# Output-gate projection first; q and k projected beside the Fourier stage and read back by the scan stage

## The chip, the cores and the metric

One core of one Trainium2 chip runs the whole kernel in one launch. The metric is the device time of that launch in microseconds (us). TensorE (PE) does the matmuls, VectorE (DVE), ScalarE (ACT) and GpSimd (POOL) the rest, and SyncE (SP) issues almost all of the transfers.

## What is computed

One encoder layer on x of 2048 positions by 1024 channels, in float32. One projection of x gives q, k (256 channels each), v (512), two gate inputs of rank 16, an output gate z_gla (512), u (512) and a second output gate z_fnet (512):

```python
proj = jnp.einsum('bsd,de->bse', x, w_in[l])
q, k, v, gf_lr, gb_lr, z_gla, u, z_fnet = jnp.split(proj, _OFFSETS, axis=-1)
```

Two branches follow. The first is gated linear attention: log decays per key channel come from the low-rank gates through log-sigmoid, a running sum of them scales q and k, and a scan over chunks goes once forward and once backward; the sum is RMS-normalised and multiplied by silu(z_gla). The second takes the real part of a two-dimensional Fourier transform of u (positions by channels in four groups), a small matrix per group, and multiplies by silu(z_fnet). Both go through one output projection, then `x <- LayerNorm(alpha * x + y)`.

## The kernel before

**Precision.** Every float32 operand of a large product is split into a rounded high part and the remainder (`split`, L53 to L59): ACT casts the high part (L56), and another engine, DVE unless the caller names one, subtracts it for the low part (L59). A product is then three matmuls: high by high, high by low, low by high. `load_x` (L72) loads one block of x, 256 positions, in two halves and splits them into two tiles `xhl` (four buffers in all, so two blocks); `proj_t` (L83) and `proj_n` (L90) run a projection of a block, the first with channels on the partitions, the second with positions there.

**Stage 1** (`phase1`, L137): the projections to u and z_fnet, in a seven-product (Strassen-like) form. A pair of 256-position blocks has fourteen products of 24 matmuls each (`run`, `product`, L304), and there are four pairs. The weights of a product are sums of quarters of the weight matrix, so someone has to form these sums and split them: `w_sums` (L170) does it, for u on DVE and for z_fnet on POOL. The order of the start is written out in `first`: pair 0 and the first products of pair 1 are woven together while weights and sums arrive. At the end of the stage the weights of the output gate z_gla are loaded and split into the buffer `wC`.

**Stage 2** (`phase2`, L424): the Fourier transform (a radix stage on DVE and POOL, L447 to L459; small matmuls L552 and L572; the product with silu(z_fnet) on POOL, L587), woven with the projection of z_gla, `zg_block` (L527): per block 96 matmuls (L87) out of `wC`, silu and scale on ACT, a store to DRAM. x comes by `load_x(b, nc.gpsimd)`: its low part is subtracted on POOL. The weights of v and of the gates are loaded into `wA` (L644, L645).

**Stage 3** (`phase3`, L661), called the scan stage below, goes over eight blocks. In block b it projects gates and v (`pw_part`, `pv_part`, L94), turns the gates into running sums and exponentials (`gates`: a matmul L722, ACT L724 to L727, DVE L728, two scans L733 and L735 over 64 partitions each, DVE L739 and L740, ACT L750 and L751), projects q and k (`qk`, 96 matmuls L87 out of `wB`), and multiplies them by the exponentials straight out of PSUM (`scaled`, L758, eight DVE operations of 64 partitions). For the block before, `gla_a` forms masked scores (PE L773 and L774, a transpose L777, a mask and a predicated copy on DVE, L779 and L780) and `gla_b` the state update and the inner output (PE L790 and L797). `chain_f` carries the state from chunk to chunk in two steps on POOL (L982, L985). x is loaded again, its low part now on DVE.

**Stage 4** (`phase4`): the output projection (L1006), norms and stores.

Each engine works through its own queue in order; the order within a queue is set by a scheduler that works from the program's order and from when buffers come free.

## Time and profile before

| | |
|---|---|
| median of 3 runs | 825.47 us (825.43 to 826.39) |
| span of the profiled execution | 823.8 us |
| PE busy | 768.0 us (93%) |
| DVE busy | 554.5 us (67%) |
| ACT busy | 352.8 us (43%) |
| POOL busy | 283.9 us (34%) |
| mean granted TensorE clock | 0.977 |
| moved by DMA | 110.57 MB |

The span runs from the first to the last instruction on the core; the median lies 1.7 us above it. The times are device times, and the three runs lie within 1 us. A busy PE is not always a useful PE: at the lower of its two clocks the same matmul counts twice the time.

### The profile page before, as it was taken

To read this page: it belongs to the slowest core of one execution; us is meant where nothing else is said; L and a number is where in the kernel's file an instruction comes from. 1 tells how busy PE (TensorE), PEld (TensorE's weight loads), DVE (VectorE), ACT (ScalarE), POOL (GpSimd) and SP (SyncE) were. 2 spreads that over 40 slices of the span, in tenths; PEclk is the share of its full clock that TensorE was granted. 3 is DMA by queue.
4 is the path that set the end of the run, shared out by engine and by line. 5 is a ranking of instruction groups with operands and counts; after the bars stand their busy time and mean duration, and the time that the engine had idled before them with its cause. 6 is when DMAs were issued, how large, how long until landed. Compare 5 with 4: busy or idle time off the path is not lost.

```text
span 823.8 us, 13935 instructions
## 1 busy us (share of the span) xinstructions
PE 768.0 (93%) x5542; PEld 721.3 (88%) x5542; DVE 554.5 (67%) x814; ACT 352.8 (43%) x635; POOL 283.9 (34%) x194
## 2 busy tenths in 40 slices
PE   6787999998859899989999999999998999999995
PEld 6787999998859799979999999999986788888884
DVE  4997757448997742357764765765775877677664
ACT  4632333235335455454344434443564343443441
POOL 0874212134446357601112111111243645545421
PEclk9999999999979999989999999999999999999998
DMA  8333552258645466762112112112165554455222
GB/s 289 105 100 123 168 166 65 94 170 249 181 130 170 131 183 184 236 204 77 53 52 103 53 52 103 52 53 78 52 200 195 194 178 160 151 175 179 88 92 81
DMA packets 61824, 110.57 MB, mean 134 GB/s; under 512 B 6228, under 2 KB 36948, under 8 KB 61751
## 3 DMA queue, kind: packets, MB, share of 16 engines
q1 hardware_dynamic: 61750, 109.60, 40.3%
q8 instruction: 45, 0.74, 0.4%
q14 instruction: 29, 0.23, 0.1%
HBM read 77.08 MB, written 32.51 MB: 133 GB/s over the span
## 4 chain that ended last, share of the span: by engine, by line
PE 50%; DMA 2%; DVE 1%; issue 1%; POOL 1%; ACT 1%; SPq 0%; POOLq 0%; DVEq 0%
PE mm L1006 19%; PE mm L87 11%; PE mm L94 10%; PE pa L773 2%; PE pg L797 2%; PE pg L790 2%; PE pa L1046 1%; DMA zg<-zg_d 1%; PE pg L777 1%; DMA wraw<-in_w_out_dram 1%; PE mm L722 1%; PE pg L1058 0%; PE pg L1059 0%; DMA qp<-q_d 0%; POOL zg L1065 0%
## 5 line engine op out<-in xcount | busy, mean ns | idle before, releaser
L982 POOL TENSOR_TENSOR S<-S 64x512 f32<-64x512 f32 x30 | 39.5, 1318 | 215.5 <-ACT S L792 210.7
L87 PE MATMUL mm<-xhl,wC_w 128*128 128x256 f32 x768 | 99.9, 290 | 2.9 <-POOL xhl L59 2.9
L94 PE MATMUL mm<-wA_w,xhl 128*128 128x272 f32 x768 | 101.2, 290 | 0.0
L87 PEld LDWEIGHTS mm<-xhl,wC_w 128*128 128x128 f32 x768 | 97.4, 199 | 3.6 <-POOL xhl L59 3.1
L1006 PE MATMUL mm<-wB_w,mix 128*128 128x512 f32 (+1 forms) x396 | 94.8, 389 | 3.5 <-ACT mix L56 2.4
L94 PEld LDWEIGHTS mm<-wA_w,xhl 128*128 128x128 f32 x768 | 97.6, 188 | 0.0
L87 PE MATMUL mm<-xhl,wB_w 128*128 128x256 f32 x768 | 97.1, 288 | 0.0
L87 PEld LDWEIGHTS mm<-xhl,wB_w 128*128 128x128 f32 x768 | 95.3, 196 | 0.0
L1006 PE MATMUL mm<-wA_w,mix 128*128 128x512 f32 (+1 forms) x396 | 92.9, 388 | 0.0
L1006 PEld LDWEIGHTS mm<-wB_w,mix 128*128 128x128 f32 x396 | 73.4, 191 | 20.4 <-ACT mix L56 3.1
L1006 PEld LDWEIGHTS mm<-wA_w,mix 128*128 128x128 f32 x396 | 71.6, 188 | 13.6
L304 PE MATMUL mm<-wC_s,x 128*128 128x256 f32 x384 | 54.2, 299 | 12.3 <-DVE x L58 4.4
L304 PEld LDWEIGHTS mm<-wC_s,x 128*128 128x128 f32 x384 | 50.8, 203 | 14.2 <-ACT wC_s L56 4.4
L1094 POOL TENSOR_TENSOR r<-r,lnb 128x1024 f32<-128x1024 f32 x15 | 35.9, 2391 | 78.2 <-issue 51.2
L59 POOL TENSOR_TENSOR xhl<-xraw,xhl 128x1024 fp32r<-128x1024 f32 x16 | 41.8, 2621 | 45.0 <-ACT xhl L56 36.0
L56 ACT CAST xhl<-xraw 128x1024 fp32r<-128x1024 f32 x32 | 33.4, 1047 | 40.8 <-PE mm L94 22.1
L59 DVE TENSOR_TENSOR x<-xraw,x 128x1024 fp32r<-128x1024 f32 (+1 forms) x29 | 39.5, 1374 | 13.5 <-ACT x L56 13.4
L56 ACT CAST x<-xraw 128x1024 fp32r<-128x1024 f32 (+1 forms) x28 | 26.9, 979 | 42.3 <-PE mm L304 22.8
L985 POOL TENSOR_TENSOR S<-S,alpha 64x512 f32<-64x512 f32 x30 | 36.4, 1214 | 2.4
L758 DVE TENSOR_TENSOR kp<-g,mm 64x512 f32<-64x512 f32 x32 | 21.9, 686 | 22.3 <-PE mm L87 20.9
L304 PE MATMUL mm<-x,wB_s 128*128 128x256 f32 x288 | 36.4, 283 | 0.0
L304 PEld LDWEIGHTS mm<-x,wB_s 128*128 128x128 f32 x288 | 35.4, 192 | 0.0
(195 smaller groups left out, 1463.1 us busy)
## 6 DMA issues: line engine op xcount, KB each, us to landing
xraw<-in_xt_dram SPq DMA_DIRECT2D x47, 512.0 KB, 4.6
xr<-in_x_dram SPq DMA_DIRECT2D x16, 512.0 KB, 3.8
out_dram<-r SPq DMA_DIRECT2D x15, 512.0 KB, 2.8
zg_d<-zs SPq DMA_DIRECT2D x32, 128.0 KB, 3.9
zfl<-zf_d SPq DMA_DIRECT2D x32, 128.0 KB, 3.0
mf_d<-yf SPq DMA_DIRECT2D x16, 256.0 KB, 2.4
wraw<-in_w_out_dram SPq DMA_DIRECT2D x16, 256.0 KB, 3.4
mf<-mf_d SPq DMA_DIRECT2D x8, 512.0 KB, 4.4
```

The source lines that it names most:

```text
L56: nc.scalar.copy(out=hi, in_=src)
L59: (lo_eng or nc.vector).tensor_tensor(out=lo, in0=src, in1=f32(hi), op=ALU.subtract)
L87: self.nc.tensor.matmul(ps, w[:, s, k, c0:c0 + P], x[:, m, k % 4, :], start=(k == 0 and i == 0), stop=(k == KB - 1 and i == 2))
L94: self.nc.tensor.matmul(ps, x[:, s, k % 4, t * P:(t + 1) * P], w[:, m, k, c0:c0 + cols], start=(k == 0 and i == 0), stop=(k == KB - 1 and ...
L304: nc.tensor.matmul(ps[:, i], s_[s][:, k, i * P:(i + 1) * P], m_[m][:, k], start=(k == 0 and j == 0), stop=(k == 3 and j == 2))
L758: V.tensor_tensor(out=o[ds, par::2], in0=e[ds, par::2], in1=ps[64 * par:64 * par + 64], op=ALU.mult)
L773: nc.tensor.matmul(af[:, h], k[0:64, h, ts_], q[0:64, h, ts_], start=True, stop=True)
L790: nc.tensor.matmul(up[:, h * P:(h + 1) * P], ks[:, h], v[:, h * P:(h + 1) * P], start=True, stop=True)
L982: E.tensor_tensor(out=S[ds, dst], in0=S[ds, dst], in1=S[ds, src], op=ALU.add)
L985: E.tensor_tensor(out=d3, in0=d3, in1=al, op=ALU.mult)
L1006: nc.tensor.matmul(y, c["mix"][:, s, eb], w[:, v, eb % 4, lo:lo + m], start=(eb == 4 and i == 0), stop=(eb == 3 and i == 2))
L1094: nc.gpsimd.tensor_tensor(out=r, in0=r, in1=lnb, op=ALU.add)
```

## The change

**Stage 1** begins with the output-gate projection. `zg_first` loads block 0 of x and the gate's weights piece by piece and runs 96 matmuls (L229) as the pieces come; `zg_block` runs the other seven blocks (672 matmuls, L87) with silu, scale and store. Beside them `w_prep` forms and splits the sums of the Strassen weights, now all on DVE; only the last four sums wait (`w_late`) until the buffer `wA`, which holds the gate's weights, is free. Then the four pairs run one after the other in the same order, and the woven start is gone. The weights of q and k are loaded into `wC` at the end of stage 1.

**Stage 2** weaves the projection of q and k (`qk_block`, 768 matmuls) where that of z_gla stood. The result is copied from PSUM by ACT and stored in DRAM by DMAs that ACT issues, instead of silu, scale and a store by SP.

**Stage 3** no longer projects q and k. Four DMAs per block (`qk_load`) bring them back, each row onto both partition halves; `scaled` becomes two DVE operations of 128 x 1024 elements whose operands both lie in SBUF (L777). x is loaded further ahead, its low part on POOL. The order of the rest is another: both gate projections first, then the gates, the earlier block's scores, and the v projections between them. Blocks 0 and 1 have their v projections earlier.

The number of matmuls is the same; 768 of them change place with 768 others.

```diff
+            def w_prep(rp):
...
+                for u in range(2):
...
+                    w_split(u, 1, RW[u, 0])
+                    yield
+                    w_split(u, 2, RW[u, 2])
+                    yield
+                    for h in range(2):
+                        sub(T[h], r(1, h), r(0, h))
+                        sub(T[2 + h], r(3, h), T[h])
+                    yield
+                    w_half(u, 6, 1)
...
+            def zg_first():
+                w = self.wzg = self.wpool.tile([P, 2, KB, 512], F32R, name="wA_w", tag="wA")
...
+                for k in range(KB):
...
+                    nc.sync.dma_start(out=xr[:, k % 4], in_=a["xt"][0, :, k])
+                    raw = self.xpool.tile([P, 512], F32, name="wraw", tag="wraw", bufs=4)
+                    nc.sync.dma_start(out=raw, in_=a["w_zg"][:, k])
...
+                    self.split(x[:, 0, k % 4], x[:, 1, k % 4], xr[:, k % 4])
+                    self.split(w[:, 0, k], w[:, 1, k], raw)
...
+                ps = zg_first()
+                xn = self.load_x(1)
+                for c in range(4):
+                    zg_out(0, c, ps[c], rp)
+                for b in range(1, NBLK - 1):
+                    xh, xn = xn, self.load_x(b + 1)
+                    zg_block(b, xh, bg, rp)
...
-            for p, c in first(xs[0], xs[1]):
-                for u in range(2):
-                    run(u, c, p, xs[p])
...
+            nxt = x_prep(0, xs[0])
+            zg_block(NBLK - 1, xn, nxt, st)
+            w_late()
+            for p in range(NP):
...
-                        self.wzg = self.load_w("wC", a["w_zg"], KB, 512)
+                        self.wqk = self.load_w("wC", a["w_qk"], KB, 512)
...
+            def qk_block(b, xh):
+                for c0, d in ((256, self.kr_d[b]), (0, self.qr_d[b])):
+                    ps = self.mm([P, 2, BLK])
+                    for i in range(2):
+                        self.proj_t(ps[:, i], xh, self.wqk, c0 + i * P)
...
+                    self.last_ev = nc.scalar.copy(out=qe, in_=ps)
+                    nc.scalar.dma_start(out=d, in_=qe)
...
-            def scaled(o, e, ps):
-                for par in range(2):
+            def qk_load(b, blk):
...
+                for o, d in ((blk["q"], self.qr_d[b]), (blk["k"], self.kr_d[b])):
                     for dr in range(2):
...
-                        V.tensor_tensor(out=o[ds, par::2], in0=e[ds, par::2], in1=ps[64 * par:64 * par + 64], op=ALU.mult)
...
+                        nc.sync.dma_start(out=o[64 * dr:64 * dr + 64].rearrange("d (i p) t -> d i p t", p=2),
+                                          in_=d.rearrange("(p d) i t -> d i p t", p=2))
...
+            def scaled(blk):
+                for n in "kq":
+                    V.tensor_tensor(out=blk[n], in0=blk[n], in1=blk["e" + n], op=ALU.mult)
...
+            prev, xn = None, self.load_x(0, nc.gpsimd)
             for b in range(NBLK):
...
                 pw_part(xh, 0, blk)
+                pw_part(xh, 1, blk)
+                gates(b, blk)
+                qk_load(b, blk)
+                if b + 1 < NBLK:
+                    xn = self.load_x(b + 1, nc.gpsimd)
...
                 if prev:
                     gla_a(b - 1, 0, prev)
...
+                    if b > 1:
+                        pv_part(xh, 0, blk)
+                    gla_b(b - 1, 0, prev)
+                scaled(blk)
                 alphas(b)
                 if prev:
                     gla_a(b - 1, 1, prev)
...
+                    pv_part(xh, 1, blk)
                     gla_b(b - 1, 1, prev)
                     self.chain_f(2 * b - 2, 2 * b)
```

**How the queues change.** First the start of DVE's queue. Before, it holds splits of x and of weights, PSUM sums (L358), sums of x (L220) and of weights (L170):

```order
L59 TENSOR_TENSOR w_115<-raww,w_114 128x1024
L59 TENSOR_TENSOR x<-x 128x1024
L358 TENSOR_TENSOR t_246<-mm,t_174 128x512
L220 TENSOR_TENSOR xraw<-xraw 128x1024 x2
L358 TENSOR_TENSOR t_274<-mm,t_201 128x512
L170 TENSOR_TENSOR ws<-raww 128x512 x2
L170 TENSOR_TENSOR ws<-raww,ws 128x512 x2
L59 TENSOR_TENSOR x<-xraw,x 128x1024
```

Now, from the first pieces of the gate projection on (xhl is x, wA_w the gate's weights; wC_s, wB_s and the sums ws, L179, are of the Strassen weights, which no matmul needs yet):

```order
L59 TENSOR_TENSOR xhl<-xraw,xhl 128x256
L59 TENSOR_TENSOR wA_w<-wraw,wA_w 128x512
L59 TENSOR_TENSOR xhl<-xraw,xhl 128x1024
L59 TENSOR_TENSOR wC_s<-raww,wC_s 128x1024
L59 TENSOR_TENSOR xhl<-xraw,xhl 128x1024
L59 TENSOR_TENSOR wC_s<-raww,wC_s 128x1024
L59 TENSOR_TENSOR xhl<-xraw,xhl 128x1024
L179 TENSOR_TENSOR ws<-raww 128x512 x2
L59 TENSOR_TENSOR wC_s<-ws,wC_s 128x512 x2
```

The sums no longer stand between a matmul and the x that it waits for, and the POOL half of them has moved here too.

Second, DVE in a middle block of the scan stage. Before:

```order
L779 TENSOR_TENSOR at<-pa,mf 128x512
L728 SCALAR_TENSOR_TENSOR g<-mm,g 128x512 x2
L780 COPY_PREDICATED at<-mb,pa 128x512
L733 SCALAR_TENSOR_TENSOR c<-rst,g 64x1024
L735 SCALAR_TENSOR_TENSOR c<-rst,g 64x1024
L739 TENSOR_TENSOR g<-c 128x1024
L744 COPY cmid<-c 128x8
L740 TENSOR_SCALAR g<-g 128x1024
```

Now (L744 and L746 are the scans, L750 and L751 what L739 and L740 were; L791 and L792 the mask and the predicated copy):

```order
L739 SCALAR_TENSOR_TENSOR g<-mm,g 128x512 x2
L744 SCALAR_TENSOR_TENSOR c<-rst,g 64x1024
L746 SCALAR_TENSOR_TENSOR c<-rst,g 64x1024
L750 TENSOR_TENSOR g<-c 128x1024
L755 COPY cmid<-c 128x8
L791 TENSOR_TENSOR at<-pa,mf 128x512
L751 TENSOR_SCALAR g<-g 128x1024
L792 COPY_PREDICATED at<-mb,pa 128x512
```

The mask of the second chunk's scores has moved from before the scans to behind them.

Third, PE in a middle block of the same stage. Before, from the transpose of the second chunk's k:

```order
L777 MATMUL pg<-ident,kp 128x128 x4
L87 MATMUL mm<-xhl,wB_w 128x256 x48
L790 MATMUL pg<-v,ks 128x128 x4
L797 MATMUL pg<-at,v 128x128 x4
L94 MATMUL mm<-wA_w,xhl 128x272 x24
L87 MATMUL mm<-xhl,wB_w 128x256 x48
L94 MATMUL mm<-wA_w,xhl 128x272 x48
```

Now (L802 and L809 are what L790 and L797 were, L725 the transpose of the gates):

```order
L789 MATMUL pg<-ident,kx 128x128 x4
L94 MATMUL mm<-wA_w,xhl 128x272 x24
L802 MATMUL pg<-v,ks 128x128 x4
L809 MATMUL pg<-at,v 128x128 x4
L94 MATMUL mm<-wA_w,xhl 128x272 x48
L725 MATMUL pg<-ident,rn 96x128
```

24 matmuls of v stand before L809, where 48 of the q projection stood before L797. On POOL, which before has only the pairs L982 and L985 in this stretch, the order in a middle block is now two pairs of state steps, each followed by one low part of x.

## Rows read from the trace of the kernel before

**Rows 1.** The page, part 1: busy time, share of the span, instructions.

```profile
PE 768.0 (93%) x5542; PEld 721.3 (88%) x5542; DVE 554.5 (67%) x814; ACT 352.8 (43%) x635; POOL 283.9 (34%) x194
```

**Rows 2.** Two 20-us windows: busy time by engine, granted clock, DMA share, GB/s.

```profile
20.00:40.00 20.00, 16.45 (x122) 15.94 (x120) 19.90 (x14) 12.52 (x18) 15.50 (x8) 0.91 0.34 114
220.00:240.00 20.00, 13.00 (x74) 12.20 (x74) 19.28 (x40) 9.82 (x20) 9.39 (x3) 0.74 0.62 193
```

**Rows 3.** Timeline of PE, start of stage 1: start, duration, instructions, idle before.

```profile
4.38 2.26 PE L304 MATMUL mm<-wC_s,x 128*128 128x256 f32 x6 [4.38 <-DVE x L58]
...
32.85 3.92 PE L304 MATMUL mm<-wC_s,x 128*128 128x256 f32 x22 [3.54 <-DVE x L59]
...
72.13 4.48 PE L304 MATMUL mm<-wA_s,x 128*128 128x256 f32 x24 [5.09 <-DVE t L371]
76.45 3.04 PE L304 MATMUL mm<-x,wA_s 128*128 128x256 f32 x24
79.33 0.87 PE L304 MATMUL mm<-wC_s,x 128*128 128x256 f32 x5
```

**Rows 4.** Timeline of DVE, start of stage 1.

```profile
9.37 0.42 DVE L59 TENSOR_TENSOR x<-xraw,x 128x256 fp32r<-128x256 f32 x1 [0.78 <-ACT x L56]
...
18.00 1.22 DVE L59 TENSOR_TENSOR x<-x 128x1024 fp32r<-128x1024 f32 x1
...
24.87 3.50 DVE L170 TENSOR_TENSOR ws<-raww,ws 128x512 f32<-128x512 f32 x2
28.29 2.30 DVE L59 TENSOR_TENSOR x<-xraw,x 128x1024 fp32r<-128x1024 f32 x1
```

**Rows 5.** Timeline of PE, scan stage: its first block, then a middle one.

```profile
361.35 0.51 PE L714 MATMUL pg<-ident,rn 128*96 128x128 f32 x2 [3.00 <-DVE rn L690]
...
363.81 13.86 PE L87 MATMUL mm<-xhl,wB_w 128*128 128x256 f32 x96
...
450.63 0.74 PE L722 MATMUL mm<-R,wg 98*128 98x256 f32 x4
...
469.86 6.19 PE L94 MATMUL mm<-wA_w,xhl 128*128 128x272 f32 x48
...
482.27 0.74 PE L722 MATMUL mm<-R,wg 98*128 98x256 f32 x4
```

**Rows 6.** Timeline of DVE, the same middle block.

```profile
453.16 0.69 DVE L779 TENSOR_TENSOR at<-pa,mf 128x512 f32<-128x512 f32 x1 [1.34 <-PE pa L774]
...
455.55 0.73 DVE L780 COPY_PREDICATED at<-mb,pa 128x512 f32<-128x512 uint8 x1
456.17 2.27 DVE L733 TENSOR_TENSOR_SCAN c<-rst,g 64x1024 f32<-64x1024 bf16 x1
458.46 2.29 DVE L735 TENSOR_TENSOR_SCAN c<-rst,g 64x1024 f32<-64x1024 bf16 x1
460.78 1.23 DVE L739 TENSOR_TENSOR g<-c 128x1024 f32<-128x1024 f32 x1
...
462.04 0.69 DVE L740 TENSOR_SCALAR g<-g 128x1024 f32<-128x1024 f32 x1
...
463.92 2.79 DVE L758 TENSOR_TENSOR qp<-c,mm 64x512 f32<-64x512 f32 x4
```

**Rows 7.** Timeline of POOL, the same middle block.

```profile
465.86 1.29 POOL L982 TENSOR_TENSOR S<-S 64x512 f32<-64x512 f32 x1 [12.41 <-ACT S L792]
467.23 1.04 POOL L985 TENSOR_TENSOR S<-S,alpha 64x512 f32<-64x512 f32 x1
```

**Rows 8.** Timeline of DVE, two places in stage 2 and one in stage 4.

```profile
204.40 9.05 DVE L59 TENSOR_TENSOR bhl<-fw,bhl 128x512 fp32r<-128x512 f32 x4
...
239.32 0.67 DVE L59 TENSOR_TENSOR bhl<-fw,bhl 128x512 fp32r<-128x512 f32 x1
...
605.01 2.87 DVE L59 TENSOR_TENSOR wA_w<-wraw,wA_w 128x512 fp32r<-128x512 f32 x2
```

**Rows 9.** Timeline of POOL in stage 2, beside the first of Rows 8.

```profile
209.46 2.84 POOL L59 TENSOR_TENSOR xhl<-xraw,xhl 128x1024 fp32r<-128x1024 f32 x1
```

More of the change, by code (lines that the diff above doesn't have):

```diff
@@ new lines, in w_prep, with load, sub @@
+            def w_prep(rp):
+                RW = {}
+                def load(u, qs):
+                    for q in qs:
+                        RW[u, q] = rp.tile([P, 4, BLK], F32, name="raww", tag="raww", bufs=6)
+                        nc.sync.dma_start(out=RW[u, q], in_=src[u][:, q // 2 * 4:q // 2 * 4 + 4, q % 2 * BLK:(q % 2 + 1) * BLK])
+                load(0, (0, 2, 1, 3))
+                load(1, (0, 2))
+                for u in range(2):
+                    T = ts[u]
+                    r = lambda q, h: RW[u, q][:, 2 * h:2 * h + 2]
+                    def sub(o, x, y):
+                        V.tensor_tensor(out=o, in0=x, in1=y, op=SUB)
+                    w_split(u, 1, RW[u, 0])
[7 more added lines that the diff above has]
+                    w_half(u, 6, 1)
+                    yield
+                    w_half(u, 5, 0)
+                    yield
+                    for h in range(2):
+                        sub(T[h], r(3, h), r(1, h))
+                        sub(T[2 + h], T[2 + h], r(2, h))
+                    yield
+                    w_split(u, 3, RW[u, 3])
+                    if u == 0:
+                        load(1, (1, 3))
+                    yield
@@ new lines, in zg_out, with zg_block @@
+            def zg_out(b, c, ps, zp):
+                zs = zp.tile([P, BLK], F32, name="zs", tag=f"t{c}")
+                nc.scalar.activation(out=zs, in_=ps, func=AF.Silu)
+                nc.scalar.activation(out=zs, in_=zs, func=AF.Copy, scale=self.gn[:, c:c + 1])
+                nc.sync.dma_start(out=self.zg_d[b][:, c], in_=zs)
+            def zg_block(b, xh, bg, zp):
+                for c in range(4):
+                    ps = self.mm([P, BLK])
+                    self.proj_t(ps, xh, self.wzg, c * P)
+                    zg_out(b, c, ps, zp)
+                    next(bg, None)
@@ new lines, in phase1 @@
+            with ExitStack() as rctx:
+                rp = self.pool("praw", ctx=rctx)
+                bg = w_prep(rp)
+                ps = zg_first()
+                xn = self.load_x(1)
+                for c in range(4):
+                    zg_out(0, c, ps[c], rp)
+                for b in range(1, NBLK - 1):
+                    xh, xn = xn, self.load_x(b + 1)
+                    zg_block(b, xh, bg, rp)
+                for _ in bg:
+                    pass
+            st = self.pool("p1", ctx=ctx)
@@ L624, in zg_all @@
                         xn = self.load_x(b + 1, nc.gpsimd)
-                    yield from zg_block(b, xh)
-            ga, gb = zg_all(), fnet_pe()
+                    yield from qk_block(b, xh)
+            ga, gb = qk_all(), fnet_pe()
             def wvg_load():
```

181 lines of the change are left out of this document (44 added, 137 removed).

## The prediction

> **What bounds the kernel now.** I read the page first: PE is busy for 93% of the span [rows 1], so the time is PE's work plus the places where PE has nothing to do or runs at its lower clock. The number of matmuls does not change, so only those places can move. The windows show two of them. From 20 to 40 us PE is busy for 16.45 of 20 us, DVE for 19.90 and POOL for 15.50; from 220 to 240 us PE is busy for 13.00 at a granted clock of 0.74, with DVE at 19.28 [rows 2]. Both times DVE is full: PE waits there for what DVE makes. PE's timeline names the waits of the start: 3.54 us for a split of x, 5.09 for a sum, and a product that took 4.48 after such a wait where the next took 2.88, start to start (76.45 to 79.33) [rows 3]. In the scan stage a middle block takes 31.64 us from L722 to L722 (450.63 to 482.27) [rows 5] and PE does not wait in it.
>
> **1. The start: about -18 us.** By 79.33 us PE had done 18 products of 2.88 us [rows 3], which is 51.8 us of work; 27.5 us were lost. DVE shows why: sums of weights stand in front of the splits of x that PE waits for, and while POOL forms its own sums each takes longer (1.75 us each in the pair at 24.87; the split of x behind it 2.30, where one at 18.00 took 1.22) [rows 4]. In the changed kernel no matmul needs a sum until the gate projection is done, and POOL forms none.
> What is still lost: the first matmul now waits for two casts on ACT one after the other, where DVE and ACT shared them, so I put it at 5.2 us instead of 4.38. Block 0 has 96 matmuls at 0.12 us (2.88 by 24), 11.5 us. Its supply holds: twelve matmuls, 1.44 us, need a split of 128x256 and one of 128x512 on DVE, 0.42 [rows 4] and about 0.69 (the mask of the same size [rows 6]). At the lower clock 24 matmuls cost 1.6 us more (4.48 against 2.88 [rows 3]); one to two such stretches make 2 to 3.5. Block 1's second half of x is cast behind two silus of block 0, about 1.2. Later blocks: DVE has 2.4 us of x per block, and for all seven together six splits of 1.22, sixteen sums of about 0.65 and eight half splits of 0.69, some 23 us; that is 40 us of work in 80. So 8 to 10 us are lost and 18 gained. Bounds: 12 if two waits like those of 3.54 and 5.09 return, 20 if none does.
>
> **2. Into the seven-product stage: +0.5 us** (0 to 2). The last four sums are cast and split when block 7 of the gate is done. On ACT these casts stand ahead of copies that free PSUM; PE has four products, 4 x 2.88 = 11.5 us, before it would miss them, about as long as ACT and DVE take for them and for the x splits between.
>
> **3. Stage 2: +0.5 us** (-1 to 3). As many matmuls stand between the Fourier parts as before. A load of x comes later in SP's queue, behind stores, and PE may wait for it earlier; but DVE is full in that stretch (19.28 of 20 [rows 2]) and the next wait, for DVE, gets shorter by as much. Sixteen copies on ACT for 32 silus and 32 scalings, and 16 stores that ACT issues, cost nothing: ACT is busy for 9.82 of 20 there. If ACT's queue fell behind, PE would wait for PSUM.
>
> **4. The edge to the scan stage: +1 us** (-2 to 4). POOL gets two to four low parts of x beside the last weights of v.
>
> **5. The scan stage: +24 us.** Taking out q and k leaves 31.64 - 96 x 0.12 = 20.1 us of PE work per block. What ran beside those 11.5 us must now run beside less. The chain that decides is on DVE, between the gates (L722) and the second mask and predicated copy, which the second inner output (L809) needs. From the rows of the middle block: L722 ends at 451.4; without the predicated copy in between, the first scan can start at 455.55, 4.2 later; the scans take 4.6 (456.17 to 460.78), the subtraction and a small copy 1.3 (to 462.04), then mask 0.69, clip 0.69, predicated copy 0.73 [rows 6]: 12.2, or 12.7 with the gaps between. PE has until then: 20.1 less the two gate projections (48 matmuls, 6.1 [rows 5]), the scores and transposes before L722 (1.7) and L809 itself (0.9), so 11.4. It waits 1.3 us in each block. Before, the q projection filled this.
> To that comes POOL. The two state steps, 1.29 and 1.04 us [rows 7], become ready just when the scans run. Before, they ran beside masks and `scaled`, whose PSUM input left them alone: four in 2.79 [rows 6]. Where POOL works on SBUF while DVE works on two SBUF operands, the trace shows both waiting: four splits took 9.05 us, 2.26 each, where one alone took 0.67 [rows 8], and POOL's operations between them 2.84 [rows 9]; two weight splits beside a pair of state steps took 2.87 [rows 8], where one alone takes about 0.69. The two engines go in turn. So one step falls between the scans and one behind them, and the chain gets longer by 1.29 + 1.04 = 2.3: the wait is 3.6 us. No row shows a scan beside POOL; its price lies between 0 and 2.3, and I take 2.3, since a scan too reads two operands from SBUF (rst and g).
> The sum: seven blocks wait, 7 x 3.6 = 25 (7 x 1.3 = 9 without POOL). Block 1 waits about 5 for q and k of block 0: they are ready some 16.5 after L722 (12.7, small copies, and two multiplications of about 1.2 each), and v and gate projections cover 12.2. After block 7 its own q and k are late by 4, of which the output projection covers 2.5: 1.5. About 1 at the first gates. Together 32.5, or 16.5. Before, the first block lost about 8: a wait of 3.00, 13.86 for 96 matmuls of 11.5 [rows 5], and smaller ones. So +24, or +8.
> `scaled` itself costs nothing on PE in the middle: two operations of about 1.2 end before the next two gate projections do. The low parts of x on POOL are made a block ahead.
> The page on SBUF of the Trainium skill (SBUF — State Buffer, section "Who interferes with whom") says that a DVE instruction with two SBUF inputs contends with a GpSimd instruction that reads SBUF, and that whoever issues first holds the shared ports for the whole instruction. By that rule the scans are blocked, and the block gets 2.3 us longer; without it 0. For splits this trace agrees (2.26 against 0.67); for a scan no row here shows it.
>
> **The sum.** -18 + 0.5 + 0.5 + 1 + 24 = +8. Against the profiled execution, 823.8 + 8 = 831.8 us; that execution lies 1.7 below the median of the runs, so I forecast **833.5 us**. The likeliest case's own range is 827 to 840.
>
> **The rivals.** (a) *Scans and state steps do not hold each other up.* For it: a scan reads narrow data (bf16) as one operand and takes 2.2 ns an element, so it leaves gaps; against it: all splits of this trace that met POOL were stretched. Then part 5 is +8: 823.8 - 8 + 1.7 = **817.5 us**, faster. The point that decides: whether L746 starts right when L744 ends.
> (b) *One of the two steps falls behind the chain.* If DVE goes from scan to scan without giving way, only the subtraction waits; 1.2 us per block instead of 2.3, eight us less: **825.5 us**.
> (c) *The start gains only 10.* If loads of x for the next block stand behind 512 KB of raw weights and PE's clock falls again after each wait, part 1 gives 10 instead of 18, with part 5 as forecast: **841.5 us**. Against it: DVE has half of its time free there.
> That the change does not do what it says is excluded by the queues: the q and k matmuls have left the scan stage in PE's queue, and the gate's stand first.
>
> **How the numbers follow.** Forecast 45%, (a) 34%, (b) 12%, (c) 9%. The measurement tells 0.2%, that is 823.8 to 827.1, from no change. Faster: nearly all of (a), a third of (b), little of the forecast: 0.39. Same: a third of (b) and the edges of both big cases: 0.11. Slower: 0.50. Cases of both signs hold most of the chance, so the range has to reach from (a) to the forecast's upper bound: 814 to 840.
>
> **What would show it.** Part 1: PE goes from about 20 us on without waits above 1 us, and the first product of the seven-product stage (L320) starts near 102 us, since 92.2 us of gate projection stand before it. Part 5: blocks of about 24 us from L733 to L733 (21.6 in case (a)), a wait of 3 to 4 us before L809 put down to DVE's predicated copy, L746 starting over 1 us after L744 ends with L984 in between, and 2.3 us for a scan alone. Wrong in the reasoning would be: waits elsewhere in the block (for q and k, for x), or a start that still loses more than 12 us.

## The result, and the profile after

The changed kernel takes **864.12 us** (median of 4 runs, 860.85 to 867.47); the kernel before, run beside it, 825.93 (4 runs, 825.43 to 826.89). The ratio is **1.0464, interval 1.0432 to 1.0497**: slower. The forecast was 833.5 us with a range of 814 to 840, so its direction was the likelier one given (0.50 for slower, 0.39 for faster), and the time lies well outside. The profiled executions are 859.1 us and 823.8 us long, 35.3 apart.

First the page's part 1 of the kernel after (busy us, share of the span and instructions of each engine), against [rows 1]:

```profile
PE 788.5 (92%) x5542; PEld 737.1 (86%) x5542; DVE 561.5 (65%) x782; ACT 381.7 (44%) x668; POOL 309.1 (36%) x193
```

PE has the same number of matmuls to do, yet it is busy for 788.5 us, where it was for 768.0. So of 35.3 us some 20.5 are matmuls that took longer (the mean granted clock is 0.955, before 0.977), and 14.8 are time without work. Where they lie is read from the windows of the two kernels, cut at the same four places of the program (stage 1 with the first projection and the seven products; stage 2; edge and scan stage; rest). The columns are the window, its sum, busy us of PE, PEld, DVE, ACT and POOL, the granted clock, the DMA share and GB/s. Before:

```profile
0.00:188.80 188.80, 170.01 (x1344) 167.82 (x1345) 127.87 (x125) 70.80 (x100) 63.05 (x39) 0.98 0.45 146
188.80:346.10 157.30, 139.11 (x1086) 136.53 (x1086) 106.71 (x207) 74.66 (x154) 85.28 (x59) 0.95 0.58 177
346.10:611.50 265.40, 260.87 (x2172) 252.27 (x2170) 174.85 (x278) 123.33 (x237) 38.10 (x38) 0.99 0.25 86
611.50:823.80 212.30, 198.00 (x945) 164.63 (x944) 145.10 (x205) 84.01 (x147) 97.45 (x61) 0.98 0.44 153
```

After:

```profile
0.00:264.40 264.40, 258.49 (x2111) 257.29 (x2112) 143.16 (x165) 117.82 (x189) 26.41 (x21) 1.00 0.49 155
264.40:421.50 157.10, 140.35 (x1088) 137.60 (x1087) 103.70 (x204) 61.64 (x108) 86.90 (x58) 0.93 0.60 181
421.50:648.10 226.60, 193.22 (x1412) 178.81 (x1410) 169.16 (x210) 119.05 (x227) 98.06 (x57) 0.89 0.42 128
648.10:859.10 211.00, 196.48 (x939) 163.40 (x938) 145.51 (x204) 83.20 (x146) 97.73 (x61) 0.98 0.44 153
```

In effect 768 matmuls of 0.12 us, 92.2 us, have gone from the third window to the first. With that taken out:

| stretch | before to after, less the moved 92.2 us | difference | forecast |
|---|---|---|---|
| stage 1 | 188.8 + 92.2 = 281.0 to 264.4 | **-16.6** | -17.5 |
| stage 2 | 157.3 to 157.1 | -0.2 | +0.5 |
| edge and scan stage | 265.4 - 92.2 = 173.2 to 226.6 | **+53.4** | +25 |
| rest | 212.3 to 211.0 | -1.3 | 0 |

The miss lies in one row. There PE is idle for 33.4 us (226.60 - 193.22) where it was idle for 4.5, 28.9 more; and its matmuls, 260.87 - 92.2 = 168.7 us of them before, now take 193.2, **24.5 us more**, at a granted clock of 0.89 in place of 0.99. The clock ratio alone makes 168.7 x 0.99 / 0.89 = 187.7, 19 of the 24.5; the other 5.5 it does not account for.

The same row by place, both stages cut at each block's first gate matmul (L722 before, L733 after), with 11.5 us of q and k taken out of each block before. The forecast is split by the terms of its part 4 and part 5:

| stretch | before, less the moved work, to after | difference | forecast | idle PE, before to after |
|---|---|---|---|---|
| edge and block 0 | 29.7 to 39.6 | **+9.9** | 1 + 1 - 8 = -6 | 3.9 to 13.6 |
| block 1 | 20.1 to 28.5 | +8.3 | 3.6 + 5 = +8.6 | 0 to 2.6 |
| blocks 2 to 6 | 100.6 to 126.2 | **+25.6** | 5 x 3.6 = +18 | 0 to 12.9 |
| block 7 | 22.8 to 32.3 | +9.5 | 3.6 + 1.5 = +5.1 | 0.6 to 4.2 |

(The forecasts add up to 25.7; the prediction rounded.) Sixteen of the 28 us that were missed lie at the edge and in block 0. What idle time does not explain is slower matmuls: 0.3 us in the first stretch, 5.7, 12.7 and 5.9 in the others.

**The start.** PE's first rows after, against [rows 3]:

```profile
4.85 3.02 PE L229 MATMUL mm<-xhl,wA_w 128*128 128x256 f32 x12 [4.85 <-ACT wA_w L56]
8.38 13.04 PE L229 MATMUL mm<-xhl,wA_w 128*128 128x256 f32 x84 [0.51 <-ACT wA_w L56]
21.93 81.36 PE L87 MATMUL mm<-xhl,wA_w 128*128 128x256 f32 x672 [0.50 <-ACT zs L235]
103.12 3.04 PE L320 MATMUL mm<-wC_s,x 128*128 128x256 f32 x24
```

After 0.5 us at 21.93 PE does 672 matmuls without a gap, and the first product starts at 103.12 (forecast 102): 103.12 - 92.16 = 11.0 us are lost, where 27.5 were.

**A middle block of the scan stage.** PE's rows after, from one L725 to the second inner output (of rows alike, and of the score matmuls, none are shown), against [rows 5]:

```profile
510.70 0.27 PE L725 MATMUL pg<-ident,rn 128*96 128x128 f32 x1
514.02 0.29 PE L725 MATMUL pg<-ident,rn 128*96 128x128 f32 x1 [2.41 <-DVE rn L702]
514.88 0.74 PE L733 MATMUL mm<-R,wg 98*128 98x256 f32 x4
...
516.74 4.43 PE L94 MATMUL mm<-wA_w,xhl 128*128 128x272 f32 x24
...
524.40 3.27 PE L94 MATMUL mm<-wA_w,xhl 128*128 128x272 f32 x24
...
529.18 1.13 PE L809 MATMUL pg<-at,v 128*128 128x128 f32 x8 [0.63 <-DVE cend L756]
```

The window of this block, from L733 to the next L733 (the columns as above):

```profile
514.88:540.76 25.88, 22.83 (x176) 21.49 (x175) 21.47 (x24) 14.22 (x27) 12.89 (x6) 0.92 0.40 126
```

The 25.88 us are 20.1 of work, as forecast, 3.05 of waits (25.88 - 22.83; 3.6 were forecast) and 2.7 of matmuls that take longer: of two equal runs of 24, the one behind the wait of 2.41 took 4.43, the other 3.27. The wait before L809, forecast as 3.6, is 0.63; the other, 2.41 before L725, was not forecast at all. The blocks last 22.9, 28.5, 25.3, 25.9, 25.7, 26.1, 23.3 and 32.3 us.

The short wait before L809 has a reason: PE itself came late, by the slower matmuls. In block 2, at a granted clock of 1.00, PE comes to L809 at 501.77, 11.4 us after the end of L733 as forecast, and waits 1.96 (for the predicated copy L792, which ends at 503.58; the row names a small copy behind it):

```profile
503.73 1.13 PE L809 MATMUL pg<-at,v 128*128 128x128 f32 x8 [1.96 <-DVE cend L756]
```

What PE waits for in the block at 514.88 stands in DVE's rows, against [rows 6]:

```profile
511.12 2.66 DVE L701 COPY rn<-rn 128x32 f32<-128x32 f32 x1 [0.65 <-ACT rn L700]
...
519.52 2.28 DVE L744 TENSOR_TENSOR_SCAN c<-rst,g 64x1024 f32<-64x1024 bf16 x1
521.82 2.29 DVE L746 TENSOR_TENSOR_SCAN c<-rst,g 64x1024 f32<-64x1024 bf16 x1
524.14 2.14 DVE L750 TENSOR_TENSOR g<-c 128x1024 f32<-128x1024 f32 x1
526.20 1.01 DVE L755 COPY cmid<-c 128x8 f32<-128x8 f32 x1
```

and in POOL's, against [rows 7]:

```profile
511.41 2.33 POOL L59 TENSOR_TENSOR xhl<-xraw,xhl 128x1024 fp32r<-128x1024 f32 x1
...
522.82 2.37 POOL L984 TENSOR_TENSOR S<-S 64x512 f32<-64x512 f32 x1 [9.08 <-ACT S L804]
525.27 1.91 POOL L987 TENSOR_TENSOR S<-S,alpha 64x512 f32<-64x512 f32 x1
```

A copy of 128x32 (L701), 0.17 to 0.18 us where POOL is quiet, takes 2.66: it begins 0.3 us before the end of a state step and ends with the low part of x that POOL forms next. PE's gate transposes hang on it. The two scans run back to back; L984, ready only 1.0 us after the second scan has begun, takes 2.37 where [rows 7] had 1.29, and then the subtraction and the small copy take 2.14 and 1.01.

In block 2 the step is ready 0.5 us before the first scan ends. These are DVE's scans and POOL's steps there:

```profile
494.25 2.28 DVE L744 TENSOR_TENSOR_SCAN c<-rst,g 64x1024 f32<-64x1024 bf16 x1
496.55 3.20 DVE L746 TENSOR_TENSOR_SCAN c<-rst,g 64x1024 f32<-64x1024 bf16 x1
```

```profile
496.04 1.56 POOL L984 TENSOR_TENSOR S<-S 64x512 f32<-64x512 f32 x1 [8.45 <-ACT S L804]
497.68 2.91 POOL L987 TENSOR_TENSOR S<-S,alpha 64x512 f32<-64x512 f32 x1
```

L984 ends at 497.60, and the second scan, whose row begins at 496.55, is longer by 0.91. So the row of a held-up scan begins as early as that of a free one, and only its length tells of the wait. It is so in blocks 2 and 7; in blocks 1 and 3 to 6 the step comes inside the second scan, as in the rows above.

**The edge.** PE's wait before the first gate transpose, after:

```profile
424.60 4.77 PE L94 MATMUL mm<-wA_w,xhl 128*128 128x272 f32 x34 [1.16 <-POOL xhl L59]
436.55 0.42 PE L725 MATMUL pg<-ident,rn 128*96 128x128 f32 x1 [7.17 <-DVE fone L872]
```

The engine that the second row names was long done. ACT's rows of the same stretch show the late one:

```profile
428.54 1.05 ACT L56 CAST xhl<-xraw 128x1024 fp32r<-128x1024 f32 x1 [11.47 <-DMA xraw<-in_xt_dram]
429.49 0.58 ACT L544 COPY qe<-mm 128x512 f32<-128x512 f32 x1
430.44 1.05 ACT L56 CAST xhl<-xraw 128x1024 fp32r<-128x1024 f32 x1 [0.37 <-DMA xraw<-in_xt_dram]
430.51 0.33 ACTq L545 DMA_DIRECT2D qr_d<-qe  x1
435.25 0.18 ACT L700 CAST rn<-mm 128x32 fp32r<-128x32 f32 x1 [3.76 <-DMA qr_d<-qe]
```

SP's queue has the load of x behind two stores of the Fourier result:

```profile
419.61 2.96 SPq L601 DMA_DIRECT2D mf_d<-yf  x2
423.59 1.32 SPq L77 DMA_DIRECT2D xraw<-in_xt_dram  x2
```

ACT waits 11.47 for that load, the copy of the last q stands behind that, and the first gate's cast (L700) waits for the store of that copy. Before, PE waited 3.00 at this place [rows 5].

### The profile page after: what moved, and what is told of

It reads as the page before. It is cut to its first block, busy times and chain, and to the rows that moved or that the text cites. A ratio compares the mean times of both kernels' runs of the same rounds, so it can differ in the third digit from the quotient of the medians.

```text
span 859.1 us, 14088 instructions
## 1 busy us (share of the span) xinstructions
PE 788.5 (92%) x5542; PEld 737.1 (86%) x5542; DVE 561.5 (65%) x782; ACT 381.7 (44%) x668; POOL 309.1 (36%) x193
## 5 line engine op out<-in xcount | busy, mean ns | idle before, releaser
L94 PE MATMUL mm<-wA_w,xhl 128*128 128x272 f32 x768 | 111.6, 306 | 1.2 <-POOL xhl L59 1.2
L59 POOL TENSOR_TENSOR xhl<-xraw,xhl 128x1024 fp32r<-128x1024 f32 x32 | 83.9, 2626 | 73.1 <-ACT xhl L56 53.5
L87 PE MATMUL mm<-xhl,wC_w 128*128 128x256 f32 x768 | 101.5, 292 | 6.1 <-POOL xhl L59 6.1
L87 PEld LDWEIGHTS mm<-xhl,wC_w 128*128 128x128 f32 x768 | 98.7, 201 | 7.2 <-POOL xhl L59 6.6
L984 POOL TENSOR_TENSOR S<-S 64x512 f32<-64x512 f32 x30 | 50.0, 1668 | 100.6 <-ACT S L804 94.8
L87 PE MATMUL mm<-xhl,wA_w 128*128 128x256 f32 x672 | 81.3, 283 | 0.5 <-ACT zs L235 0.5
L87 PEld LDWEIGHTS mm<-xhl,wA_w 128*128 128x128 f32 x672 | 80.8, 192 | 1.1 <-ACT zs L235 0.7
L382 POOL TENSOR_TENSOR t<-t,t 128x512 f32<-128x512 f32 x7 | 11.0, 1576 | 191.8 <-ACT t L381 191.8
L56 ACT CAST xhl<-xraw 128x1024 fp32r<-128x1024 f32 (+1 forms) x54 | 51.4, 951 | 50.0 <-DMA xraw<-in_xt_dram 34.1
L59 DVE TENSOR_TENSOR x<-xraw,x 128x1024 fp32r<-128x1024 f32 x28 | 37.5, 1349 | 29.6 <-ACT x L56 29.6
L56 ACT CAST x<-xraw 128x1024 fp32r<-128x1024 f32 x28 | 29.0, 1047 | 44.2 <-PE mm L320 37.5
L59 DVE TENSOR_TENSOR xhl<-xraw,xhl 128x1024 fp32r<-128x1024 f32 (+1 forms) x22 | 20.4, 932 | 28.6 <-ACT xhl L56 28.6
```

The costliest lines, as they stand in the source:

```text
L56: nc.scalar.copy(out=hi, in_=src)
L59: (lo_eng or nc.vector).tensor_tensor(out=lo, in0=src, in1=f32(hi), op=ALU.subtract)
L87: self.nc.tensor.matmul(ps, w[:, s, k, c0:c0 + P], x[:, m, k % 4, :], start=(k == 0 and i == 0), stop=(k == KB - 1 and i == 2))
L94: self.nc.tensor.matmul(ps, x[:, s, k % 4, t * P:(t + 1) * P], w[:, m, k, c0:c0 + cols], start=(k == 0 and i == 0), stop=(k == KB - 1 and ...
L984: E.tensor_tensor(out=S[ds, dst], in0=S[ds, dst], in1=S[ds, src], op=ALU.add)
```

## The experiments

Each edit is against the kernel named. All were timed against the kernel before (824.9 to 826.1 us); ratios stand with their intervals. The changed kernel's own ratio was 1.0464.

### Is it POOL?

**mid_lo_dve**: the changed kernel, the low parts of x for scan blocks 1 to 7 back on DVE.

```diff
-                    xn = self.load_x(b + 1, nc.gpsimd)
+                    xn = self.load_x(b + 1, None if b else nc.gpsimd)
```

> Changed kernel, but the low parts of x for blocks 1 to 7 of the scan stage are subtracted on DVE instead of POOL (block 0 stays on POOL). Port theory (a low part on POOL, 2.3 us, holds up DVE's small copy of the gate inputs, L701, which takes 2.66 instead of 0.18 us; PE then waits 2.4 us and runs at the lower clock for some us): L701 back to 0.2 us, the wait before L725 under 0.7 us, blocks of 22 to 23 us instead of 25.3 to 26, total 12 to 20 us below the changed kernel, 844 to 852 us. Cover theory (DVE's chain is too long for the 20 us of PE work left in a block, whoever does the low parts): DVE gets 2.5 us more per block, blocks stay at 25 to 26, total within 5 us of 864.

852.11 us, 1.0307 (1.026 to 1.0354): **12 less** than the changed kernel. DVE's rows:

```profile
505.67 0.17 DVE L701 COPY rn<-rn 128x32 f32<-128x32 f32 x1
...
514.76 3.20 DVE L746 TENSOR_TENSOR_SCAN c<-rst,g 64x1024 f32<-64x1024 bf16 x1
518.00 1.88 DVE L750 TENSOR_TENSOR g<-c 128x1024 f32<-128x1024 f32 x1
```

L701 is back at 0.17, the wait before L725 at 0.92, the blocks at 23.9 to 24.4. What is left meets the state steps: here one is ready at 514.24, inside the first scan, and the second scan takes 3.20 as in block 2 above; PE waits 1.97 before L809.

**no_pool**: mid_lo_dve with the scan stage's state steps on DVE too, so that POOL does nothing in its blocks.

```diff
-        E = self.nc.gpsimd
+        E = E or self.nc.gpsimd
...
-                self.chain_step(n + 1, n, n, 0)
+                self.chain_step(n + 1, n, n, 0, self.nc.vector)
```

> As the run with the low parts of blocks 1 to 7 on DVE (852 us), and the state steps of the scan stage (L984, L987) on DVE too: POOL does nothing there. Port theory: the subtraction L750 (2.1 us beside a state step) and the small copy L755 (1.0) go back to 1.23 and 0.16; that is 1.7 us less on the chain to L809, and its wait of 1.97 us goes to 0.3 to 1, though DVE has four operations of about 0.7 us more per block; total 838 to 850 us. If DVE's load decides rather than the port: blocks get longer by 2 us, total 855 to 870.

847.48 us, 1.0272 (1.0255 to 1.029): **16.6 less** than the changed kernel. DVE's rows, and then a window over five blocks:

```profile
516.93 1.21 DVE L750 TENSOR_TENSOR g<-c 128x1024 f32<-128x1024 f32 x1
518.06 0.16 DVE L755 COPY cmid<-c 128x8 f32<-128x8 f32 x1
```

```profile
484.40:597.10 112.70, 105.17 (x873) 98.64 (x873) 94.68 (x150) 69.87 (x135) 0.00 (x0) 1.00 0.45 137
```

Blocks last 22.7 us, with waits of about 1.0 before L809 and 0.65 before L725, and the granted clock is 1.00. Having this work on POOL and not on DVE thus cost 16.6 us; still, the kernel stays 22 us slower than the one before. By place (cut as in the table above), the edge and the scan stage are still 32.5 us longer than the old ones less the moved work: 5.9 at the edge and in block 0, 5.6 in block 1, 11.8 in blocks 2 to 6, 9.2 in block 7.

**rn_on_act**: the changed kernel, L701 on ACT instead.

```diff
-                V.tensor_copy(out=rn[:, t, 64:96], in_=rn[:, t, 0:32])
+                nc.scalar.copy(out=rn[:, t, 64:96], in_=rn[:, t, 0:32])
```

> Changed kernel, but the small copy of the gate inputs (L701) is made by ACT; low parts of x stay on POOL. Port theory: nothing on the way from the gate projections to the gates can be held up any more, except the subtraction from PSUM, which has one SBUF operand; the wait before L725 falls from 2.4 us to under 0.7, total 8 to 20 us lower. Cover theory: the wait moves elsewhere in the block, total within 5 us of 864.

857.2 us (851.7 to 858.7), 1.035 (1.0301 to 1.04). The wait before L725 is gone from the middle blocks, but another one came, for ACT:

```profile
504.72 1.53 PE L802 MATMUL pg<-v,ks 128*128 128x128 f32 x8 [2.92 <-ACT ks L794]
...
582.22 1.16 PE L802 MATMUL pg<-v,ks 128*128 128x128 f32 x8 [2.92 <-ACT ks L794]
```

The time lies between the two that were expected. The waits are alike, but what follows them is not: blocks 2 to 4 take 25.4 to 26.6 us at granted clocks of 0.87 to 0.93, blocks 5 and 6 take 23.9 at 1.00. What decides this, no run shows.

**edge_lo_dve**: only the low parts of blocks 0 and 1 on DVE.

```diff
-            prev, xn = None, self.load_x(0, nc.gpsimd)
+            prev, xn = None, self.load_x(0)
...
-                    xn = self.load_x(b + 1, nc.gpsimd)
+                    xn = self.load_x(b + 1, nc.gpsimd if b else None)
```

> Changed kernel, but only the low parts of x for blocks 0 and 1 of the scan stage go to DVE. Edge theory (POOL's queue delays these low parts, so the next buffer for x is free late, a cast of x on ACT waits for the transfer and holds up the last copies of q and their store, and the first cast of the gate inputs waits for that store): the wait of 7.17 us before the first L725 falls below 4 us, total 5 to 12 us lower than the changed kernel. If the store alone sets it, whatever POOL does: no change.

862.2 us, 1.044 (1.0403 to 1.0477): no change that the intervals tell, and the first gate waits 9.75. The low parts of x on POOL are not what makes the edge. (POOL's last products of the Fourier stage may still have a part in it: the stores ahead of the load of x wait for them. No run changes those.)

**before_lo_pool**: the kernel *before*, with the scan stage's low parts on POOL.

```diff
-                xh = self.load_x(b)
+                xh = self.load_x(b, nc.gpsimd)
```

> Kernel before, but the low parts of x in the scan stage go to POOL. Port theory: DVE's small copies (L690) are held up as in the changed kernel where they meet a low part; the block gets 1 to 4 us longer, total 833 to 855 us. Cover theory (the q and k projections cover such delays): total within 3 us of 826.

826.55 us, 1.0013 (0.9991 to 1.0035): nothing. Blocks stay at 31.6 to 31.7. A DVE copy there is stretched to 1.19 us too, and PE does not wait for it. The same contention is free while q and k stand in the block.

### The edge and the chain

**edge_buf**: the changed kernel, the last block's q copy in a buffer of its own, so that nothing waits for its store.

```diff
-                    qe = fp.tile([P, 2, BLK], F32, name="qe", tag="qe", bufs=2)
+                    if b < NBLK - 1:
+                        qe = fp.tile([P, 2, BLK], F32, name="qe", tag="qe", bufs=2)
+                    else:
+                        qe = self.xpool.tile([P, 2, BLK], F32, name="qe", tag="wraw", bufs=4)
```

> Changed kernel, but the last block's copies of k and q before their store (L544) go into a buffer that stage 3 does not lay other tiles over. Store theory (the first cast of the gate inputs, L700, waits at the edge until the store of the last q has left the buffer whose place it takes, 435.25 where the store is issued at 430.5): L700 4 to 5 us earlier, the wait of 7.17 us on PE before the first L725 falls to 2 to 3, total 4 to 9 us below the changed kernel, 855 to 860 us. Queue theory (ACT's own order, with casts of x that wait for a late transfer ahead of it, sets the start of L700 anyway): at most 1 us earlier, total within 3 us.

861.83 us, 1.0447 (1.0426 to 1.0468). L700 runs at 431.20 in place of 435.25, and the first gates come 11.9 us after the edge in place of 16.7. The next gates still wait, 5.21 where they waited 4.39:

```profile
432.98 0.42 PE L728 MATMUL pg<-ident,rn 128*96 128x128 f32 x1 [3.20 <-DVE rn L705]
...
455.33 0.42 PE L728 MATMUL pg<-ident,rn 128*96 128x128 f32 x1 [5.21 <-DVE rn L705]
```

From the edge to the end of the scan stage the trace is 3.9 us shorter, but this execution reached the edge 2.1 later and took 2.0 longer behind the stage. The times do not tell the run from the changed kernel. The pair all_three and mask_early, below, does.

**mask_early**: mid_lo_dve with the gates' second half put behind the predicated copy.

```diff
+                    gla_a(b - 1, 1, prev)
+                gates2(b, blk, prev)
...
-                    gla_a(b - 1, 1, prev)
```

(`gates2`, not shown, holds the second half of `gates`, issued after the copy.)

> As the run with the low parts of blocks 1 to 7 on DVE (852 us), but the scores of the second chunk are masked before the subtraction that follows the scans (L750), not behind it; DVE's work is the same. Chain theory (L809 waits for the mask, 2 us per block, as the covering q projection is gone): that wait goes to under 0.3 us, blocks from 23.9 to 21 to 22.5 us, total 836 to 846 us. Rival (the wait turns up again at q and k or at the gates): total within 4 us of 852.

852.52 us, 1.0327 (1.0307 to 1.0348), against 852.11 without it. The profiled execution was the slowest of five (858.39). In it the wait before L809 falls from 1.97 to 0.42 and stands before L725 instead:

```profile
503.62 1.13 PE L816 MATMUL pg<-at,v 128*128 128x128 f32 x8 [0.42 <-DVE at L799]
...
513.28 0.28 PE L725 MATMUL pg<-ident,rn 128*96 128x128 f32 x1 [2.52 <-DVE rn L702]
```

(L816 is L809 of the changed kernel.) This change of order inside the block gains nothing.

**all_three** (mid_lo_dve, mask_early and edge_buf) and **all_four** (also the state steps on DVE):

> Low parts of blocks 1 to 7 on DVE, second mask before the subtraction, and the buffer of the last copies kept. If the three costs are separate they add: 852 less 6 to 16 less 4 to 9, 828 to 842 us. If they overlap (what one saves waits at the next): 840 to 850 us.

> Changed kernel with low parts of blocks 1 to 7 and the state steps on DVE, the second mask before the subtraction, and the buffer of the last copies kept. From the parts: 847.5 (POOL idle in the scan stage) less 2 to 7 for the mask and 0 to 5 for the buffer: 836 to 846 us. Still above the kernel before, since blocks 0 and 1 and the two ends of the stage remain as they are.

848.18 us, 1.0277 (1.0256 to 1.0299), and 846.08, 1.0247 (1.0219 to 1.0274). all_three differs from mask_early by the buffer alone and is 4 us faster, with intervals that lie apart: there the buffer is worth 4 us. all_four is within 1.4 us of no_pool alone, and 20 us remain.

### What were q and k worth where they stood?

**extra_96**: the changed kernel, with 96 matmuls in each of blocks 1 to 7 whose result is thrown away, 80.6 us of PE work in the place of q and k.

```diff
+            def extra(xh, c0):
+                ps = self.mm([P, 2, BLK])
+                for i in range(2):
+                    self.proj_t(ps[:, i], xh, wvg, c0 + i * P)
...
+                    extra(xh, 0)
...
+                    extra(xh, 256)
```

> Changed kernel, and in blocks 1 to 7 of the scan stage 96 more matmuls of the size of a q and k projection stand where those stood before (weights of v, the product is thrown away): 672 matmuls, 80.6 us of work at full rate. Cover theory (a block waits for a chain on DVE, ACT and POOL whose length does not depend on PE's work): blocks go from 25.5 to 31.6 to 33 us, the time that they had with q and k, total 35 to 55 us above the changed kernel, 899 to 919. Rival (waits are where they are, whatever PE does beside them): 75 to 81 us more, 939 to 945.

909.96 us (906.4 to 914.2), 1.1013: 46 more, not 80.6. A window over three blocks:

```profile
502.70:599.00 96.30, 96.30 (x812) 93.12 (x812) 51.71 (x72) 44.01 (x81) 34.62 (x18) 1.00 0.32 100
```

PE is busy without a gap at a granted clock of 1.00, in blocks of 32.0 us. So 80.6 us of PE work cost 46 in this stage; the other 35 took the place of waits and slow matmuls.

**before_short_qk**: the other way round, the kernel before with q and k cut from 96 matmuls a block to 12.

```diff
-                    self.proj_t(ps[:, i], xh, w, c0 + i * P)
+                    for j in range(3):
+                        nc.tensor.matmul(ps[:, i], w[:, 0, 0, c0 + i * P:c0 + (i + 1) * P], xh[0][:, 0, 0, :],
+                                         start=(j == 0), stop=(j == 2))
```

> Kernel before, with its own order and with x's low parts on DVE, but q and k are projected by 12 matmuls per block instead of 96 (the rest is left out): 80.6 us less work. Cover theory (without q and k the block is bound by the chain from the gates, in the old order too): blocks of 24 to 26 us instead of 21.6, total 20 to 36 us above 745, that is 765 to 781. Rival (the old order leaves no wait, the new order does): blocks of 21.6 to 22.5, total 745 to 755.

799.0 us, 0.9685 (0.9654 to 0.9717): 26 less than the kernel before in the same comparison (824.97), for 80.6 us of work taken out. Blocks take 27.5 us where 21.6 were to be had:

```profile
412.00:550.00 138.00, 124.17 (x927) 115.44 (x927) 103.38 (x160) 68.80 (x135) 25.01 (x20) 0.93 0.20 74
```

That is more than either expectation gave (765 to 781, 745 to 755). So the loss does not come from the new order alone: in the old one it is larger.

**extra_24**: the changed kernel with 24 thrown-away matmuls a block (20.2 us in all), ahead of the transposes of L725.

```diff
+                    if b > 0:
+                        dm = self.mm([P, BLK])
+                        for j in range(12):
+                            nc.tensor.matmul(dm, wvg[:, 0, 0, 0:P], xh[0][:, 0, 0, :], start=(j == 0), stop=(j == 11))
                     nc.tensor.transpose(tp[0:96, t], rn[:, t], ident)
```

> Changed kernel, and in blocks 1 to 7 of the scan stage 24 more matmuls (result thrown away), twelve ahead of each transpose of the gate inputs (L725): 168 matmuls, 20.2 us at full rate. Clock theory (the wait of 2.4 us before L725 also costs the time after it, since the granted clock falls): the added work fills the wait and the clock stays up, blocks of 24 to 26 us, total within 6 us of the changed kernel's 864. Without it: 12 to 20 us more.

884.75 us (881.9 to 886.2), 1.0713: 20.6 more, all of their own time. The wait before L725 is gone, but the copy `ks` on ACT now comes behind an exponential, and PE waits 2.83 us before the products that read it. So this run does not tell what filling the wait alone would give; that stays open.

### Only a part of the move

**hybrid2, hybrid3, hybrid4**: the first NF blocks of the gate projection first, the others beside the Fourier stage; q and k stay in the scan stage as before. All but hybrid2 also spread the gate's blocks further out over the Fourier stage, and **hybrid4_early_v** and **hybrid5_early_v** load the weights of v earlier. The core of the edit against the changed kernel:

```diff
+NF = 4
...
-                for b in range(1, NBLK - 1):
+                for b in range(1, NF - 1):
...
-            def qk_all():
-                xn = self.load_x(0, nc.gpsimd)
-                for b in range(NBLK):
+            def zg_all():
+                xn = self.load_x(NF, nc.gpsimd)
+                for b in range(NF, NBLK):
```

> Stage 1 of the changed kernel with only blocks 0 and 1 of the output gate ahead of the seven-product stage, the other six beside the Fourier stage as before, scan stage of the kernel before. Start theory (the gain at the start is there by itself, 16.5 us, and what made the change slower is the scan stage): the weight sums, some 23 us on DVE besides x, find only 23 us of cover, so about 8 to 12 us are gained at the start; the Fourier stage loses 23 us of cover of which it has 18 us of waits to begin with, 2 to 6 us lost: 815 to 823 us. Rival (the Fourier stage loses as much as the start gains): 823 to 832.

> As before with three blocks of the output gate first and five beside the Fourier stage, spread out there. Start theory: 14 to 16 us gained at the start, 5 to 9 lost in the Fourier stage, 814 to 822 us. Rival: 824 to 835.

> As before with four blocks first and four beside the Fourier stage. Start theory: 16 us gained, 10 to 18 lost, 818 to 828 us. Rival: 828 to 845.

> Four blocks of the output gate first, four beside the Fourier stage, scan stage of the kernel before, and the weights of v loaded and split earlier in the Fourier stage (in the run with four blocks PE reached the scan stage at 338.3 us and waited there for these weights until 356, first gates at 373.4: 35 us where the kernel before takes 17). Start theory: the edge falls back to 17 to 22 us, total 13 to 18 us lower, 816 to 822 us, faster than before. Rival (Fourier stage is bound by DVE, PE then waits inside it): 826 to 836.

> As before with five blocks of the output gate first and three beside the Fourier stage. Start theory: up to 4 us more gained at the start, 3 to 8 more lost in the Fourier stage: 816 to 828 us. Rival: 830 to 840.

841.47 (1.0173), 842.59 (1.0208), **834.57** (1.01, 1.0075 to 1.0124), 835.11 (1.0107) and 834.32 us (1.0108). hybrid2 and hybrid3 lie above both of their expected ranges (in hybrid2 PE waits 12.48 us before the first of the seven products), the other three inside that of the rival. From the first gates on, hybrid4's scan stage takes 248.8 us, as before. Its stage 1 ends at 226.0, where the old one with that work added would end at 189.0 + 46.1 = 235.1: 9 us gained, not 16. And stage 2 and the edge, 157.1 + 16.7 = 173.8 us before, take 112.3 + 35.1 = 147.4: taking 46.1 us of PE work out of the Fourier stage shortens it by 26. With early weights it is 147.8, with five blocks 138.8 (35 for 57.6). So stage 2 and the edge lose 20 us (147.4 + 46.1 - 173.8) where the start gains 9: the gate's matmuls are cover in the Fourier stage as well. No version beat the kernel before.

## Why the prediction was wrong

**Part 1, the start, was right.** -16.6 us were measured for the whole of stage 1, -17.5 forecast for it (parts 1 and 2); 11.0 us are lost at the start where 8 to 10 were put, within its bounds. **Parts 2 and 3 were right**: no wait in the seven products' window beyond the gap at 21.93, and -0.2 in stage 2.

**Part 4, the edge, and part 5's credit for the first block failed.** +1 was forecast for the edge and +1 for the first gates, and "about 8" us that the old first block lost were taken as gone: together -6, and +9.9 was measured. PE idles there for 13.6 us where it idled for 3.9, and its matmuls are as slow as before, so the 8 did not come back. The prediction looked at POOL's low parts; edge_lo_dve shows that they are not the cause. The two queues made the wait before the first gates: the load of x behind stores in SP's, the last q's copy and store behind the late cast in ACT's. The prediction's part 3 had seen the late load and put it before another wait. Freeing the store is worth about 4 us (all_three against mask_early). What else makes blocks 0 and 1 longer stays open, and so does block 7, where +9.5 came and +5.1 was forecast: no run took these apart.

**Part 5, the middle blocks, failed** in two ways.

*The wait's place and size.* "One step falls between the scans and one behind them" came out in blocks 2 and 7 alone; in the others the step was not ready when the first scan ended. The prediction's test, whether L746 starts right when L744 ends, could not tell: the row starts 0.02 us later in either case. The size was too large: 2.3 us were put, and the chain gets longer by 3.20 - 2.29 + 1.88 - 1.21 = 1.6 where the step is early (L750 takes 1.88 there) and by 2.14 + 1.01 - 1.21 - 0.16 = 1.8 where it is late, between rival (b) and the forecast. PE's share until L809 was right, 11.4; the wait at full clock is 1.96 (block 2), not 3.6. And the low parts of x, priced at nothing because they "are made a block ahead", stretch L701, which decides when the gates start: 2.41 of 3.05 us of waiting in the block at 514.88 are there. `scaled`, put at two operations of 1.2, is stretched by a low part too (3.21 for the second, at 505.97), but ACT's cast ahead of L701 ends later still, so PE does not feel it. Waits elsewhere in the block were named as what would prove the reasoning wrong. That the idle time of the whole stage agrees, 33.4 us measured and 32.5 + 1 forecast, is luck: by the places of the table 2, 8.6, 18 and 5.1 were forecast, and 13.6, 2.6, 12.9 and 4.2 came. By the Trainium skill's page "SBUF — State Buffer", section "Who interferes with whom", copies too can take the shared ports and whoever issues first holds them. The copy L755 agrees (1.01 against 0.16, ending with the state step that began before it). L701 agrees only in that it is held up: its row begins 0.3 us before the low part's, and yet it ends with the low part. The prediction applied the rule to the scans, and not to the small copies.

*The clock.* The sum of part 5 counted each new wait by its length alone. **This is the term that is missing**: PE's matmuls in the stage took 24.5 us longer, at a granted clock of 0.89, and that is, by kind, nearly all of the 28 us between +25 and +53. Part 1 had priced just this (1.6 us for 24 matmuls behind a wait, from [rows 3]); in a block the same thing is there to read, 4.43 against 3.27. In most experiments the two go together: with POOL quiet the waits fall to about 1 us and the blocks' granted clock is 1.00; with the hole filled (extra_96) it is 1.00 too; with the waits of before_short_qk, 1.78 before its scores among them, it is 0.93. But not every wait is followed by slow matmuls (1.96 in block 2 and some of 2.92 in rn_on_act are not), and the run that was to fill the wait, extra_24, moved it to another place. So that the waits lowered the clock is read from rows, and not shown by a run.

Behind both stands what the forecast's frame left out. It began from "the number of matmuls does not change, so only those places can move", and took 92.2 us out of the scan stage as if they could leave nearly whole. extra_96 puts a price on it: 80.6 us of PE work there cost 46, because without it a middle block does not fall to its 20.1 us of work but to 25 or 26, and to 22.7 with POOL quiet. POOL's part of that is shown to be 16.6 us; the 22 that remain in no_pool are not one removable wait: two of the waits taken away (rn_on_act, mask_early) came back wholly or in part elsewhere, and most of what remains of the stage's loss lies in its first two blocks and its last.

## What to carry to other kernels

Matmuls that run beside a chain of other engines are worth, when moved, only what their stage does not need as cover: compare PE's work that stays with the chain that stays, and look at each operation of that chain for contention that was free before (before_lo_pool cost 0; taking the low parts of seven blocks off POOL in the changed kernel saved 12). Price a new PE wait between its length alone and its length plus the slower matmuls behind it, from a pair of equal rows with and without a wait. Price the first and the last block of a stage by themselves, and do not take their old losses as gone. If a wait that you remove comes back at another place, look for work that the stage lacks before you tune its order further.

## What was not expected of the hardware

- A copy of 128x32 on DVE, 0.17 us alone, took 2.66 beside POOL: the last 0.3 us of one elementwise operation and the whole of the next, 2.33; one of 128x8 went from 0.16 to 1.01. How small the operation is does not protect it.
- A POOL operation that is ready before a DVE scan ends gets in between it and the next scan, whose row then begins at once but takes 3.20 in place of 2.29 (block 2; mid_lo_dve). One that becomes ready inside the second scan waits for its end: L984 took 2.37 in place of 1.29.
- The granted clock of a whole stage fell to 0.89 (PE busy for 193.22 of 226.60 us); before, it was 0.99 (260.87 of 265.40). Equal waits did not always go with it: in rn_on_act blocks with the same wait of 2.92 ran at 0.87 to 0.93 and at 1.00.
